# Hybrid decoder step with 32 experts: eight neighbouring weight rows per partition, low parts off GpSimd, gathers ahead of the second split

## Chip, cores and metric

The kernel runs on one core of a Trainium2 chip. The metric is the device time of one execution in microseconds (us); the median of several runs is compared. The engines are PE (TensorE matmul; PEld is its weight load), DVE (VectorE), ACT (ScalarE), POOL (GpSimd) and SP (SyncE, which here only issues transfers). Every engine works through its own queue in order.

## What is computed

One step of a one-layer decoder on 1024 prompt tokens and 64 sample tokens (1088 rows of 1024). A combined projection feeds a recurrent head group and a dilated window attention, their outputs go through `w_out`, then comes the mixture of experts that this change is about, then a gated per-layer embedding and a last norm. The reference computes the experts densely:

```python
def expert_step(acc, ws):
    wg, wu, wd, c = ws
    out = (jax.nn.silu(hf @ wg) * (hf @ wu)) @ wd
    return acc + c[:, None] * out.astype(jnp.float32), None
# hf: the 1088 normalized rows; wg, wu [1024, 256], wd [256, 1024], 32 experts
# c: non-zero for 2 experts a token (best of 4 groups, then the best 2 of its 8)
acc, _ = lax.scan(expert_step, jnp.zeros((n, D), jnp.float32), (wg, wu, wd, comb.T))
```

## The kernel before

All products are made exact enough by splitting every operand into a high and a low part (`split`: the high part is a copy on ACT, the low part `src - hi` a subtraction on another engine), and by three matmul passes high*high, high*low and low*high (`mm3`, L1283).

Stages, in order: projection and recurrent heads, attention, and then
- **phase 4** (about 960 to 1075 us of the span): nine token tiles. Each goes through `w_out`, is normalized (`norm`, L1345: `hn` is written to the table HN in DRAM, one row of 1024 per token), and routed (`route`, a chain of small DVE instructions). The last `route` ends with `idx`, the token numbers of each expert's 96 slots (L1476).
- **phase 5** (about 1088 to 1465 us): a loop over the 32 experts, software-pipelined. For expert e: `gather` (L1524, an indirect transfer issued by POOL) fetches 96 rows of HN; `xt` transposes them on PE, 128 columns at a time, and splits the result (`xh`, `xl`); `gu` multiplies by the gate and up weights (8 blocks of 128 rows, 24 matmuls into p4g); `act` (L1547 to L1549) makes silu(gate)*up; `ht` transposes and splits that (`hh`, `hl`); `down` multiplies by the down weights (12 matmuls into p4y), copies the two halves of the result out (L1568 on ACT, L1570 on DVE) and stores them to YE.
- **phase 6** (about 1460 us to the end): the rows of YE are fetched back per token, mixed, gated and written.

Weights of an expert arrive by `load_w` (gate and up, two transfers each for two halves, L1243 and L1244, into `wraw`) and `load_d` (down, one transfer, L1265, into `draw`), all issued by SP. Two experts' gate/up fit into `wraw`, four experts' down into `draw`; a load is issued when the split of the expert that held the buffer has read it. `split_w` (four quarters, `wh` on ACT, `wl` on DVE) and `split_d` (two halves, `dh` on ACT, `dl` on POOL) make the parts; both record their instructions on L47 (high) and L49 (low). `split_w` of expert 1 has an extra wait on `after_idx`, the instruction that writes `idx`. Which instruction stands where in an engine's queue is decided by a scheduler from the program order and its own estimate of durations.

In memory a gate or up matrix is 1024 rows of 1 KB. Block k of 128 rows (rows 128k to 128k+127) has its row 128k+p on partition p, so a partition receives four separate rows of 1 KB from one transfer. A down matrix has rows of 4 KB.

Of the kernel before, what the change touches and what calls it, by code (L numbers as in the profile page):

```python
# [29 lines left out]
XB = 4      # tiles of x in flight  # L30
# [3 lines left out]
class K:  # L34
# [9 lines left out]
    def split(self, hi, lo, src, lo_eng=None, hi_eng=None):  # L44
        """hi + lo == src exactly; hi and lo carry float32r values."""
        nc = self.nc
        (hi_eng or nc.scalar).activation(hi, src, AF.Copy) if (hi_eng or nc.scalar) is nc.scalar else hi_eng.tensor_copy(hi, src)  # L47
        e = lo_eng or nc.vector
        return e.tensor_tensor(lo, src, hi.bitcast(F32), op=ALU.subtract)  # L49

    def bcast_row(self, vec, n):
        """DRAM vector of n values as [128, n], the same on each partition."""
        return bass.AP(tensor=vec.tensor, offset=vec.offset, ap=[[0, 128], [1, n]])

    def rstd(self, pool, ss, n, width, eps, scale, tag):
        """(ss*scale + eps)^-0.5 for a [n, width] tile."""
# [16 lines left out]
    def dram(self):  # L73
# [3 lines left out]
        self.XV = t("XV", [4, 128, T])           # value, per pair of heads, channel-major  # L77
        self.ARd = t("ARd", [4, 128, 17, 128])   # per chunk: removal key | receptance, times the decay so far; last chunk: samples
        self.KB = t("KB", [4, 128, T])           # key over the decay so far
        self.BB = t("BB", [4, 128, T])           # removal key times a over the decay so far  # L80
        self.PC = t("PC", [4, 128, 24])          # decay over a chunk; 16 prompt chunks, 8 sequences
        self.BV = t("BV", [4, 128, T])           # bonus
# [3 lines left out]
        self.QP = t("QP", [2, 512, NP])          # prompt queries, channel-major, as an exact sum of two float32r parts  # L86
# [7 lines left out]
    def phase1(self):  # L94
        nc, tc, I, O = self.nc, self.tc, self.I, self.O
        with ExitStack() as es:
# [13 lines left out]
            # projection, 25 tiles of 128 columns, the lora tile first; the first two go along with the norm  # L110
# [33 lines left out]
            # last projected rows  # L144
# [7 lines left out]
    def vectors(self, c1):  # L152
        nc, I = self.nc, self.I
        nc.sync.dma_start(self.cst, I['cst'])
        # per-channel vectors, channel-major
# [23 lines left out]
        # mu * state_shift, [128, b, ct]  # L179
# [68 lines left out]
    def project(self, ct, out, chunks=range(3)):  # L248
        """columns 128 ct.. of the projection, channel-major; those of RWKV shifted by a token"""
# [28 lines left out]
    def copy(self, c, after):  # L278
        """Half of a sample's cache moves on, not before another instruction; the last rows come with the projection."""
# [33 lines left out]
    def lora(self, lora, lp):  # L313
        nc, I, vec, pm = self.nc, self.I, self.vec, self.pm1
        # contractions over 32 or 64 rows: the data's high and low parts stacked, the weights' parts in two passes
# [47 lines left out]
    def rwkv_ops(self, p, xr, xk, xv, ep):  # L363
        """per-token operands of a pair of heads: decay products within chunks, keys, bonus"""
# [7 lines left out]
        # decay so far within the chunk: before and after the token  # L372
# [17 lines left out]
        # removal key, normalized per head, negated  # L390
# [12 lines left out]
        # key  # L403
# [3 lines left out]
        # bonus  # L407
# [11 lines left out]
        # products with the decay  # L419
# [23 lines left out]
def host_consts():  # L443
    """Tables that depend on shapes alone."""
# [10 lines left out]
    # identity rows for a quarter of the columns: column 4c + d on partitions with (p // 8) % 4 == d  # L455
# [5 lines left out]
class K2(K):  # L461
# [17 lines left out]
    def pools2c(self, es):  # L479
        """tiles that stay over the RWKV stage and the samples' part of it"""  # L480
        nc = self.nc
        self.c2 = c2 = es.enter_context(self.pool("c2", side="right"))
        # zero-padded block-diagonal operands; the padding is written once
# [27 lines left out]
    def pools2a(self, es):  # L511
        """the first of pools2, opened while the projection still runs"""
# [28 lines left out]
    def phase2a(self):  # L541
        """the first chunks' systems, which the projection hides"""
# [48 lines left out]
    def pair_load(self, dst, src, t0, nck):  # L591
        """[pair, channel, token] into the block-diagonal [channel, chunk, pair, (head, token)]"""
# [5 lines left out]
    def prepA(self, u):  # L598
        """what the chunk systems and the states' first products need; two chunks, or the samples"""
# [71 lines left out]
    def solve(self, u, G):  # L671
        """(I - A)^-1 of each 64 x 64 chunk system: 32-row halves by forward substitution, joined by products.
        Partition (head of the pair, half, column mod 4, chunk and pair)."""
# [19 lines left out]
    def join(self, u, G):  # L693
        nc, sv, X = self.nc, self.sv, G['X']
        TT = G['TT'] = self.TT[u % 2]
        R1 = sv.tile([128, 8, 32], F32, tag="R1", name="R1")     # rows: [t, column / 4, (column mod 4, system)]
        RT = sv.tile([128, 8, 32], F32, tag="RT", name="RT")     # transposed: [column, system, t]
# [3 lines left out]
        # diagonal halves; systems of pairs 0, 1 on rows 0..63, of pairs 2, 3 on rows 64..127  # L701
# [26 lines left out]
    def solve_s(self, G):  # L728
        """inverse of the 8 x 8 systems, one per partition (pair, head, sequence)"""
# [62 lines left out]
    def sample2(self, G, y):  # L792
# [4 lines left out]
        for p in range(4):  # L797
            # states, rows (sequence parity, v), then turned to [(head, k), (sequence, v)]
# [28 lines left out]
            for j, (src, lhs) in enumerate(((G['Vt'][:, 0, p, :], G['Kt']), (u, G['Bt']))):  # L827
                # rows spread over their sequence
# [69 lines left out]
class K3(K2):  # L898
# [3 lines left out]
    def attn_out(self, pool, X, at, n, i0, gat, tags=("asq", "an", "ao"), bufs=1, w=512):  # L902
        """rmsnorm of [n, 512] mixed heads, then channel-major into MX[4:8]."""
# [59 lines left out]
    def head(self, h, ia, ib):  # L963
        """a head's operands for query tiles ia..ib"""
# [4 lines left out]
        # keys: high over low part; queries: either part twice  # L969
# [9 lines left out]
    def samples_out(self, pool, X, n, w):  # L979
        """the samples' heads, from rows per head to rows per token"""  # L980
# [13 lines left out]
    def phase3(self, pairs, depth, banks, hooks={}):  # L994
        nc, tc, I, O = self.nc, self.tc, self.I, self.O
        gat, at = self.gat, self.at
        with ExitStack() as es:
# [5 lines left out]
            else:       # stays for the following phases  # L1003
# [864 lines left out]
```

## Time and profile before

| | |
|---|---|
| time, median of 3 runs | 1621.02 us |
| the runs | 1618.59, 1621.02, 1627.01 us |
| span of the profiled execution | 1623.8 us |
| PE, DVE, ACT, POOL busy | 86%, 59%, 44%, 34% of the span |
| mean granted clock of TensorE | 0.932 of full speed |

No separate time was recorded for the profiled execution; its span, from its first to its last instruction, lies inside the range of the timed runs and 2.8 us above their median. Busy shares are averages over stages that differ; matmul ends are modelled, so a PE that is busy throughout is not at its peak.

### The profile page before, as it was taken

How to read it: one execution, taken by the hardware profiler on the slowest of the kernel's cores; microseconds unless marked ns; L12 is line 12 of the kernel's file. 1: busy time of each engine (PE TensorE's matmuls, PEld its weight loads, DVE VectorE, ACT ScalarE, POOL GpSimd, SP SyncE). 2: the span in 40 equal slices, each digit the busy share in tenths (PEclk: the TensorE clock that was granted, in tenths of full speed). 3: DMA queues.
4: the chain of work that ended last, by engine and by line, in shares of the span. 5: the costliest groups of instructions: out<-in, count | busy, mean ns of one | idle time of the engine just before them, and what ended most of it. 6: DMA issues, size and time to landing. Idle time of an engine off the chain costs nothing. (4 is left out here: it accounts for less than half of the span.)

```text
span 1623.8 us, 24626 instructions
## 1 busy us (share of the span) xinstructions
PE 1398.6 (86%) x9017; PEld 1159.6 (71%) x9018; DVE 960.8 (59%) x2121; ACT 722.2 (44%) x1304; POOL 549.1 (34%) x427
## 2 busy tenths in 40 slices
PE   4999999999889889973988999948988788797996
PEld 4888999999667767762867787836765455565884
DVE  7524663551476857343656534459876678686664
ACT  5535453231334435341444633327765566674332
POOL 8004651001122222431223513126675454454230
PEclk9999999999979898986999998979999899899998
DMA  6156558895774753366676566579999799996551
GB/s 200 53 177 188 153 164 284 301 348 179 200 219 138 190 162 115 90 138 156 202 209 187 157 212 213 188 246 319 340 364 336 241 309 319 319 348 220 189 183 65
DMA packets 306158, 350.02 MB, mean 216 GB/s; under 512 B 105757, under 2 KB 249951, under 8 KB 305504
## 3 DMA queue, kind: packets, MB, share of 16 engines
q1 hardware_dynamic: 261424, 287.46, 56.4%
q0 software_dynamic: 39712, 43.76, 9.7%
q10 hardware_dynamic: 4896, 17.17, 2.8%
q8 instruction: 73, 1.20, 0.3%
q14 instruction: 53, 0.43, 0.1%
HBM read 277.45 MB, written 104.33 MB: 235 GB/s over the span
## 5 line engine op out<-in xcount | busy, mean ns | idle before, releaser
L49 POOL TENSOR_TENSOR dl<-draw,dh 128x1024 fp32r<-128x1024 f32 x66 | 175.3, 2678 | 98.8 <-ACT dh L47 98.7
L264 PE MATMUL pj<-hT_hi,wh 128*128 128x384 f32 (+1 forms) x600 | 198.9, 333 | 4.7 <-DVE lora L272 2.7
L264 PE MATMUL pj<-hT_hi,wl 128*128 128x384 f32 (+1 forms) x600 | 198.6, 331 | 0.0
L264 PE MATMUL pj<-hT_lo,wh 128*128 128x384 f32 (+1 forms) x600 | 198.0, 330 | 0.0
L264 PEld LDWEIGHTS pj<-hT_hi,wh 128*128 128x128 f32 x600 | 113.4, 190 | 6.6 <-DVE lora L272 3.0
L264 PEld LDWEIGHTS pj<-hT_hi,wl 128*128 128x128 f32 x600 | 113.6, 189 | 2.4 <-issue 2.2
L264 PEld LDWEIGHTS pj<-hT_lo,wh 128*128 128x128 f32 x600 | 113.9, 190 | 0.6 <-issue 0.2
L47 ACT ACTIVATE dh<-draw 128x1024 fp32r<-128x1024 f32 x66 | 66.3, 1052 | 70.2 <-PE p4y L1283 41.2
L688 DVE TENSOR_TENSOR ftmp<-At,X 128x60 f32<-128x60 f32 (+24 forms) x248 | 59.3, 251 | 44.7 <-DMA At<-ABd 26.9
L1040 PE MATMUL pS<-k,q 128*128 128x512 f32 (+2 forms) x192 | 56.3, 401 | 33.6 <-DMA q<-QP 32.2
L1524 POOL DMA_INDIRECT x<-HN,idx x32 | 51.3, 1604 | 94.0 <-PE p4t L1534 37.8
L1069 PEld LDWEIGHTS po<-v,pt 128*128 128x128 f32 x576 | 74.2, 197 | 10.7 <-issue 2.4
L1069 PE MATMUL po<-v,pt 128*128 128x128 f32 x576 | 79.8, 284 | 1.4 <-ACT pt L1067 1.1
L1052 ACT ACTIVATE s<-s,nm 128x128 f32<-128x128 f32 (+7 forms) x64 | 49.4, 772 | 61.8 <-DVE X L744 21.3
L767 POOL TENSOR_TENSOR s<-S,pc 128x512 f32<-128x512 f32 x16 | 16.9, 1053 | 162.6 <-PE pj L264 69.9
L690 DVE TENSOR_TENSOR X<-X,ftmp 128x60 f32<-128x60 f32 (+24 forms) x248 | 59.0, 250 | 4.5
L49 DVE TENSOR_TENSOR wl<-w,wh 128x1024 fp32r<-128x1024 f32 x25 | 35.0, 1400 | 44.7 <-ACT wh L47 43.9
L1043 DVE CUSTOM_DVE_ANT_0 s<-pS,bias 128x512 f32<-128x512 f32 (+2 forms) x96 | 50.9, 552 | 17.7 <-PE pxt L1063 13.2
L1040 PEld LDWEIGHTS pS<-k,q 128*128 128x128 f32 x192 | 32.7, 208 | 39.9 <-issue 21.8
L1283 PE MATMUL p4y<-dh,hl 128*96 128x512 f32 x128 | 52.4, 409 | 5.5 <-DVE hl L49 5.5
L1067 ACT ACTIVATE pt<-pxt 128x512 f32<-128x512 f32 (+3 forms) x64 | 32.6, 512 | 54.7 <-PE pxt L1063 41.8
L1283 PE MATMUL p4y<-dh,hh 128*96 128x512 f32 x128 | 48.1, 416 | 5.5 <-ACT hh L47 5.3
(653 smaller groups left out, 3874.9 us busy)
## 6 DMA issues: line engine op xcount, KB each, us to landing
wraw<-in_w_gate_dram SPq DMA_DIRECT2D x64, 512.0 KB
wraw<-in_w_up_dram SPq DMA_DIRECT2D x64, 512.0 KB
draw<-in_w_down_dram SPq DMA_DIRECT2D x32, 1024.0 KB
out_dram<-in_cache_k_win_dram SPq DMA_DIRECT2D x16, 1016.0 KB
out_dram<-in_cache_v_win_dram SPq DMA_DIRECT2D x16, 1016.0 KB
w<-in_w_in_dram SPq DMA_DIRECT2D x25, 512.0 KB
kc<-in_cache_k_win_dram SPq DMA_DIRECT2D x48, 256.0 KB
vc<-in_cache_v_win_dram SPq DMA_DIRECT2D x48, 256.0 KB
```

The lines of the kernel that those rows point to most:

```text
L47: (hi_eng or nc.scalar).activation(hi, src, AF.Copy) if (hi_eng or nc.scalar) is nc.scalar else hi_eng.tensor_copy(hi, src)
L49: return e.tensor_tensor(lo, src, hi.bitcast(F32), op=ALU.subtract)
L264: nc.tensor.matmul(p[:, :nn], a[:, k, :], b[:, k, n0:n0 + nn], start=(m == 0), stop=(m == 23))
L688: nc.vector.tensor_tensor(o, At[:, t, t + 1:32][:, :, None].to_broadcast([128, m, c]), X[:, t, None, 0:c].to_broadcast([128, m, c]), op=AL ...
L690: nc.vector.tensor_tensor(X[:, t + 1:32, 0:c], X[:, t + 1:32, 0:c], o, op=ALU.add)
L1040: nc.tensor.matmul(ps[:, :n], q[:, a, i * 128:(i + 1) * 128], k[:, c0:c0 + n], start=(a == 0), stop=(a == 1))
L1043: nc.vector.tensor_tensor_reduce(s[:, c0:c0 + n], ps[:, :n], bias[:, bo:bo + n], 1.0, -3e38, ALU.add, ALU.max, m)
L1052: ex = nc.scalar.activation(s[:, :nb * 128], s[:, :nb * 128], AF.Exp, bias=nm, accum_out=den)
L1067: nc.scalar.activation(pt[:, b0:b0 + m, :], px[:, :m, :], AF.Copy)
L1069: nc.tensor.matmul(po, pt[:, b, :], v[:, b, :], start=(b == 0), stop=(b == nb - 1))
L1283: self.nc.tensor.matmul(p, a[x][:, k, :], w, start=(k == 0 and q == 0), stop=(k == kn - 1 and q == 2))
L1524: nc.gpsimd.indirect_dma_start(out=X[e][:n], out_offset=None, in_=self.HN, in_offset=bass.IndirectOffsetOnAxis(ap=self.idx[:, e:e + 1], ax ...
```

## The change

- `load_w` puts rows 8p to 8p+7 of a gate or up matrix on partition p: a transfer takes rows 8p+4g to 8p+4g+3, which are 4 KB in one piece in memory, to 4 KB in one piece on the partition. Block k of the product then holds rows 8p+k. `split_w` only views the buffer in that order.
- So that the data agree, `norm` writes `hn` with its columns permuted: column 128k+p holds channel 8p+k. The instruction reads `x2` and the gain with a step of 8 elements (32 bytes).
- `split_d` makes the low parts `dl` on DVE and not on POOL. In `down` both halves of the result are copied out by ACT; the DVE copy goes.
- `moe_start` issues the gathers of experts 0, 1 and 2 before expert 0's split in program order, and behind them a one-element memset on POOL; `split_w` of expert 1 waits for that memset and not for `idx`.
- The overflow path (`overflow_expert`, for an expert with over 96 tokens) reads its weights in the new order. Comments and docstrings that the new file leaves out are not shown.

```diff
 def load_w(self, j, after=(None, None), part=(0, 1)):
...
             if 0 <= j < NE:
-                self.hold(nc.sync.dma_start(t[:, :, 0:256], v(I['w_gate'][0, j])), after[g])
-                self.hold(nc.sync.dma_start(t[:, :, 256:512], v(I['w_up'][0, j])), after[g])
+                v = lambda a: a.rearrange("(p k) f -> p k f", k=KC)[:, 4 * g:4 * g + 4, :]
+                t = t.rearrange("p a b -> p (a b)").rearrange("p (s k f) -> p s k f", s=2, k=4)
+                self.hold(nc.sync.dma_start(t[:, 0], v(I['w_gate'][0, j])), after[g])
+                self.hold(nc.sync.dma_start(t[:, 1], v(I['w_up'][0, j])), after[g])
+                t = t.rearrange("p s k f -> p k s f")
...
 def split_w(self, j, q, eng=None, after=None):
...
-        self.hold(self.split(t[0], t[1], self.W[j][2][q // 2][:, o], lo_eng=eng), after)
+        src = self.W[j][2][q // 2][:, o]
+        h, l = (x.rearrange("p k (s f) -> p k s f", s=2) if 0 <= j < NE else x for x in t)
+        self.hold(self.split(h, l, src, lo_eng=eng), after)
...
 def split_d(self, j, k):
...
-        return self.split(h[:, k], l[:, k], r[:, k], lo_eng=self.nc.gpsimd)
+        return self.split(h[:, k], l[:, k], r[:, k])
...
 def norm(i):
...
-            nc.vector.scalar_tensor_tensor(hn[:n], x2[:n], r[:n], gf[:n], op0=ALU.mult, op1=ALU.mult)
+            v = lambda a: a[:n].rearrange("t (p k) -> t k p", k=KC)
+            nc.vector.scalar_tensor_tensor(hn[:n].rearrange("t (k p) -> t k p", k=KC), v(x2), r[:n], v(gf), op0=ALU.mult, op1=ALU.mult)
             nc.gpsimd.dma_start(self.HN[t0:t0 + n, :], hn[:n])
...
 def down(e):
...
-                if j:
-                    nc.scalar.activation(y[:n, c], p[:n], AF.Copy)
-                else:
-                    nc.vector.tensor_copy(y[:n, c], p[:n])
+                nc.scalar.activation(y[:n, c], p[:n], AF.Copy)
...
 def moe_start(self):
-        gather(0)
-        gather(1)
+        for e in range(3):
+            gather(e)
+        m = self.tc.keep_in_program_order(self.nc.gpsimd.memset(self.c4.tile([1, 1], F32, name="issued"), 0.0))
+        self.after_idx = m
         for q in range(4):
             self.split_w(0, q)
...
 def phase5(self):
...
         for e in range(NE + 1):
-            if e == 0:
-                gather(2)
```

POOL's queue at the start of phase 5: the gathers of experts 0 to 6 and the first low parts of down weights (`dl`), before:

```order
L1353 DMA HN<-hn 128x1024
L1524 DMA x_11024<-HN,idx 96x1024
L1524 DMA x_11026<-HN,idx 96x1024
L1524 DMA x_11070<-HN,idx 96x1024
L1524 DMA x_11121<-HN,idx 96x1024
L1524 DMA x_11197<-HN,idx 96x1024
L1524 DMA x_11299<-HN,idx 96x1024
L1524 DMA x_11401<-HN,idx 96x1024
L49 TENSOR_TENSOR dl<-draw,dh 128x1024 x2
```

and in the changed kernel (its L1532 is L1524 of before, L1361 is L1353):

```order
L1361 DMA HN<-hn 128x1024
L1532 DMA x_11024<-HN,idx 96x1024
L1532 DMA x_11026<-HN,idx 96x1024
L1532 DMA x_11028<-HN,idx 96x1024
L1585 MEMSET issued 1x1
L1532 DMA x_11123<-HN,idx 96x1024
L1532 DMA x_11199<-HN,idx 96x1024
L1532 DMA x_11301<-HN,idx 96x1024
L1532 DMA x_11403<-HN,idx 96x1024
```

The order of the gathers is the same; the memset stands behind the third, and from there to the end of phase 5 POOL has gathers alone. On DVE the four low parts of expert 1 (`wlb`) stand at the same place in both, behind the last `route` and ahead of expert 0's `xl`; only what they wait for has moved.

DVE's queue over one expert in the first third of phase 5, before (`wli` and `wlj`: low parts of gate/up, `y`: the copy of the first half of `down`'s result, `h`: the two products of `act`):

```order
L49 TENSOR_TENSOR xl<-p4t,xh 128x4x96
L1570 COPY y_11615<-p4y 96x512
L49 TENSOR_TENSOR wli<-wraw,whi 128x1024
L49 TENSOR_TENSOR hl<-p4h,hh 128x192
L1548 TENSOR_TENSOR h_11709<-p4g,h_11709 96x256
L49 TENSOR_TENSOR wli<-wraw,whi 128x1024
L49 TENSOR_TENSOR xl<-p4t,xh 128x4x96
L1549 TENSOR_TENSOR h_11709<-p4g,h_11709 96x256
L49 TENSOR_TENSOR wlj<-wraw,whj 128x1024 x2
```

and in the changed kernel (its L1556 and L1557 are L1548 and L1549 of before):

```order
L49 TENSOR_TENSOR xl<-p4t,xh 128x4x96
L49 TENSOR_TENSOR dl<-draw,dh 128x1024 x2
L49 TENSOR_TENSOR hl<-p4h,hh 128x192
L1556 TENSOR_TENSOR h_11711<-p4g,h_11711 96x256
L49 TENSOR_TENSOR wlj<-wraw,whj 128x1024
L1557 TENSOR_TENSOR h_11711<-p4g,h_11711 96x256
L49 TENSOR_TENSOR wlj<-wraw,whj 128x1024
L49 TENSOR_TENSOR xl<-p4t,xh 128x4x96
L49 TENSOR_TENSOR wlj<-wraw,whj 128x1024 x2
```

The copy is gone, and the two `dl` of the next expert stand ahead of `hl`, both products of `act` and the next expert's `wl`.

ACT's queue over the same expert in the changed kernel:

```order
L1575 ACTIVATE y_11617<-p4y 96x512
L47 ACTIVATE dh<-draw 128x1024 x2
L1575 ACTIVATE y_11617<-p4y 96x512
L47 ACTIVATE hh<-p4h 128x192
L1555 ACTIVATE h_11711<-p4g 96x256
L47 ACTIVATE whj<-wraw 128x1024
```

Before, only the second copy `y` stood there, behind `dh`; the rest has the same order. SP issues the same 64 + 64 + 32 weight transfers.

## Rows read from the trace of the kernel before

**Rows 1.** The page: the span, and busy us (share) and instructions of each engine.

```profile
span 1623.8 us, 24626 instructions
PE 1398.6 (86%) x9017; PEld 1159.6 (71%) x9018; DVE 960.8 (59%) x2121; ACT 722.2 (44%) x1304; POOL 549.1 (34%) x427
```

**Rows 2.** Busy time in stretches: start and end, length, busy us (instructions) of PE, PEld, DVE, ACT, POOL, granted clock, DMA share (over 1 where transfers overlap in an engine), GB/s. All of phase 5, its middle, and the 20 us that moved most.

```profile
1088.00:1465.00 377.00, 319.89 (x1482) 220.66 (x1482) 285.05 (x316) 243.31 (x349) 209.07 (x91) 0.93 0.95 315
1100.00:1440.00 340.00, 284.94 (x1320) 196.31 (x1320) 255.68 (x282) 216.72 (x314) 190.66 (x83) 0.93 0.97 320
1180.00:1200.00 20.00, 19.10 (x94) 13.38 (x93) 16.22 (x20) 12.31 (x19) 15.40 (x7) 1.00 1.07 362
```

**Rows 3.** Two lines of the instructions by line: the sigmoid of `act`, once an expert, with the start of its first and last; and the time that PE stood before the first matmul after the branch of `overflow` (PE's timeline: start, duration, instruction, idle time before it and what ended it).

```profile
L1547 ACT ACTIVATE h<-p4g x32: 363/380/383, 1098.4 to 1455.4; 96x256 f32<-96x256 f32 x32
...
1396.71 0.71 PE L1283 MATMUL p4g<-wha,xh 128*96 128x512 f32 x1 [7.63 <-DVEq L1641]
```

**Rows 4.** The DMA view of two short stretches, 1147 to 1150 us (only pieces of 1 KB) and 1310 to 1311.5 us (only pieces of 4 KB but for four): packets, MB, GB/s, and how many packets were how small.

```profile
DMA packets 1052, 1.04 MB, mean 348 GB/s; under 512 B 32, under 2 KB 1052, under 8 KB 1052
...
DMA packets 151, 0.60 MB, mean 403 GB/s; under 512 B 2, under 2 KB 4, under 8 KB 151
```

**Rows 5.** Issues of 1100 to 1460 us: transfer, queue, count, KB each. Those of `w_up` read like those of `w_gate`.

```profile
wraw<-in_w_gate_dram SPq DMA_DIRECT2D x54, 512.0 KB
draw<-in_w_down_dram SPq DMA_DIRECT2D x26, 1024.0 KB
YE<-y ACTq DMA_DIRECT2D x30, 384.0 KB
```

**Rows 6.** Groups of instructions of 1100 to 1440 us by line and shape: count, busy us and mean ns of one, idle time before.

```profile
L49 POOL TENSOR_TENSOR dl<-draw,dh 128x1024 fp32r<-128x1024 f32 x56 | 147.7, 2660 | 78.2 <-ACT dh L47 78.1
...
L49 DVE TENSOR_TENSOR wls<-wraw,whs 128x1024 fp32r<-128x1024 f32 x4 | 4.7, 1216 | 0.6 <-ACT whs L47 0.6
L49 DVE TENSOR_TENSOR xl<-p4t,xh 128x384 fp32r<-128x384 f32 x57 | 30.3, 544 | 3.2 <-ACT xh L47 3.2
L49 DVE TENSOR_TENSOR hl<-p4h,hh 128x192 fp32r<-128x192 f32 x29 | 10.1, 349 | 16.4 <-ACT hh L47 16.4
L1548 DVE TENSOR_TENSOR h<-p4g,h 96x256 f32<-96x256 f32 x29 | 11.9, 411 | 17.4 <-ACT h L1547 17.4
L1570 DVE COPY y<-p4y 96x512 f32<-96x512 f32 x28 | 19.0, 677 | 7.6 <-PE p4y L1283 7.4
...
L47 ACT ACTIVATE dh<-draw 128x1024 fp32r<-128x1024 f32 x56 | 56.2, 1052 | 53.4 <-PE p4y L1283 35.5 <-issue 17.8
L47 ACT ACTIVATE xh<-p4t 128x384 fp32r<-128x384 f32 x59 | 26.8, 483 | 3.9 <-PE p4t L1534 3.9
L1568 ACT ACTIVATE y<-p4y 96x512 f32<-96x512 f32 x28 | 16.1, 575 | 0.0
L1547 ACT ACTIVATE h<-p4g 96x256 f32<-96x256 f32 x29 | 10.9, 377 | 26.9 <-PE p4g L1283 26.8
L47 ACT ACTIVATE hh<-p4h 128x192 fp32r<-128x192 f32 x29 | 9.4, 323 | 30.8 <-PE p4h L1557 24.6 <-issue 4.6 <-PE p4t L1534 1.6
```

**Rows 7.** Timeline of phase 5 around 1124 us (start, duration, engine, instruction, idle time before it): four `dl` in a row on POOL, one `wl` on DVE, and PE's next matmul.

```profile
1123.88 9.44 POOL L49 TENSOR_TENSOR dl<-draw,dh 128x1024 fp32r<-128x1024 f32 x4
1125.59 8.81 DVE L49 TENSOR_TENSOR wlg<-wraw,whg 128x1024 fp32r<-128x1024 f32 x1
1136.66 0.74 PE L1283 MATMUL p4g<-whf,xl 128*96 128x512 f32 x1 [5.65 <-DVE xl L49]
```

**Rows 8.** What SP's queue waited for in phase 5 (total us, times, longest), and from ACT's timeline one `dh` that stood ready with nothing in the profile to wait for.

```profile
SPq L1265 <- POOL dl L49: 94.3, 20, 8.7
...
1212.03 2.01 ACT L47 ACTIVATE dh<-draw 128x1024 fp32r<-128x1024 f32 x2 [4.76 <-issue]
```

**Rows 9.** PE's work for one expert: ten matmuls of 512 columns in a row (the chain that ended last) and the eight transposes of `xt` (timeline).

```profile
1453.05 2.31 PE p4g L1283 x10
...
1202.44 0.82 PE L1534 MATMUL p4t<-ident,x 96*128 96x96 f32 x8
```

**Rows 10.** Timeline from the last tile of phase 4 to the first matmul of phase 5.

```profile
1065.30 1.28 DVE L1352 SCALAR_TENSOR_TENSOR hn<-x,r4r,gain 128x1024 f32<-128x1024 f32 x1 [0.74 <-POOL r4r L61]
1066.50 0.25 DVE L1373 SCALAR_TENSOR_TENSOR lgs<-p4h,r4r,rb 128x36 f32<-128x36 f32 x1
1074.74 4.61 DVE L49 TENSOR_TENSOR wlb<-wraw,whb 128x1024 fp32r<-128x1024 f32 x4
1075.47 4.75 POOL L1524 DMA_INDIRECT x<-HN,idx  x1 [8.03 <-DVE ci L1637]
1079.37 0.37 SPq L1243 DMA_DIRECT2D wraw<-in_w_gate_dram  x1
1080.53 0.92 POOL L1524 DMA_INDIRECT x<-HN,idx  x1 [0.31 <-issue]
1086.93 1.54 PE L1534 MATMUL p4t<-ident,x 96*128 96x96 f32 x8 [12.73 <-DMA x<-HN,idx]
1088.39 1.20 DVE L49 TENSOR_TENSOR xl<-p4t,xh 128x384 fp32r<-128x384 f32 x2 [9.04 <-ACT xh L47]
```

**Rows 11.** Two reductions on DVE in `route`: 96 elements read with a step of 8 elements, and 192 neighbouring ones (min/median/max ns).

```profile
L1397 DVE TENSOR_REDUCE rse<-rt x3: 316/323/340, 988.5 to 1068.1; 128x24 f32<-128x96 f32 x3
...
L1417 DVE TENSOR_REDUCE rrk<-rsl x3: 344/348/353, 1006.6 to 1072.3; 128x6 f32<-128x192 f32 x3
```

More of the change, by code (lines that the diff above doesn't have):

```diff
@@ L1650, in overflow_expert @@
         V = lambda t, w: r4.tile([128, w], F32, name="v" + t, tag=t, bufs=1)
-        wt = lambda n, k, m: I[n][0][ds(e, 1)].rearrange("o p f -> p (o f)")[128 * k:128 * k + 128 * m]
+        wt = lambda n: I[n][0][ds(e, 1)].rearrange("o p f -> p (o f)")
         for k in range(4):
             for q, n in ((0, 'w_gate'), (256, 'w_up')):
-                nc.sync.dma_start(g[k][:, :, q:q + 256], wt(n, 2 * k, 2).rearrange("(k p) f -> p k f", p=128))
+                nc.sync.dma_start(g[k][:, :, q:q + 256], wt(n).rearrange("(p k) f -> p k f", k=KC)[:, 2 * k:2 * k + 2])
         for k in range(2):
-            nc.sync.dma_start(d[k], wt('w_down', k, 1))
+            nc.sync.dma_start(d[k], wt('w_down')[128 * k:128 * k + 128])
         for i, (t0, n) in enumerate(TT):
```

## Prediction

> **What bounds the kernel now.** I first look for the stage. PE is busy 86% of the span [rows 1], but the edits touch phase 5, its start, and `norm` in phase 4, so I read phase 5 by itself: 377 us in which no engine is full, PE at 85%, DVE 76%, ACT 65%, POOL 55%, while the DMA engines show 0.95, and in the slice that moved most 1.07 at 362 GB/s [rows 2]. So transfers come nearest to a limit.
>
> What does an expert take? The first and last sigmoid lie 357.0 us apart, 31 experts, 11.52 us each. Once, PE stood 7.63 us for the branch of `overflow`, which the change leaves alone [rows 3]; without it 11.27 us.
>
> What must the DMA engines move for an expert? Gate and up 4 x 512 KB = 2.10 MB, down 1.05 MB, the store 0.39 MB [rows 5], and the gather as much as the store: 3.93 MB. Pieces of 1 KB went at 348 GB/s, pieces of 4 KB at 403 [rows 4]. Gate and up, in 1 KB pieces, take 2.10 / 348 = 6.03 us, the other 1.84 MB 4.55 us: 10.58 us. The measured 11.27 is 0.69 us or 6.5% more.
>
> That rest has a visible cause. POOL's `dl` and DVE's subtractions slow each other: a `wl` that takes 1.216 us where POOL is quiet [rows 6] took 8.81 us beside four `dl`, and PE then stood 5.65 us [rows 7]. DVE's work for an expert, unhindered, is 4 x 1.216 + 2 x 0.544 + 0.349 + 2 x 0.411 + 0.677 = 7.80 us [rows 6]; it was busy 255.7 us in 340 [rows 2], which at 11.52 us are 29.5 experts, 8.66 us each. So 0.86 us per expert is mutual slowing. And SP stood 94.3 us because the buffer of the next down matrix was still being read by `dl` [rows 8]; what stands behind that load in SP's queue waits too.
>
> **The change, part by part.**
>
> *Rows of 4 KB.* The bytes stay, the pieces of gate and up go from 1 KB to 4 KB. Both speeds are in [rows 4], so per expert 2.10 / 348 - 2.10 / 403 = 6.03 - 5.20 = 0.83 us less, and the DMA floor is 3.93 / 403 = 9.75 us. The bounds: nothing, if 403, seen over 1.5 us, is a burst that a whole phase doesn't sustain; 0.83 if it is sustained. I take the whole, since these were plain weight loads too. The Trainium skill, in "DMA: Bandwidth & Descriptors", section "Specifications", speaks against that twice: it puts full rate at pieces of 512 B or more, by which 1 KB pieces have nothing to gain, and a core's share of HBM at about 358 GB/s, by which the 403 would not last. On the first the trace disagrees (348 against 403); on the second the fastest 20 us, 362 GB/s, lie close to the page's figure, though they were moved largely in 1 KB pieces. By the page's figure an expert would take 10.98 us and the sum below would be about 1609 us.
>
> *Low parts from POOL to DVE, a copy from DVE to ACT.* DVE loses 0.677 and gains 2 x 1.216 us: 9.55 us an expert, now unhindered but for the gathers. ACT becomes 6 x 1.052 (`wh`, `dh`) + 2 x 0.483 + 0.377 + 0.323 + 2 x 0.575 = 9.13 us [rows 6], from 8.55. PE needs 36 matmuls of 0.231 us and eight transposes in 0.82: 9.14 us [rows 9], and two short transposes more. So the DMA floor of 9.75 is still the highest, but three engines stand within 0.7 us of it, where before the next engine stood 1.4 below 10.58. What the lock cost (0.86 us of DVE) goes; what comes is that `dl` stands in DVE's queue ahead of `hl` and `act`. Bounds for the net of the two: a gain of the whole 0.69 us above the floor, or a loss, worked out under rival C. I take it as zero: the excess over the floor stays 0.69 us, with another cause. An expert then takes 9.75 + 0.69 = 10.44 us, 0.83 less, and 31 of them 25.7 us.
>
> SP's wait for `dl` should shrink, since DVE makes it 1.2 us after `dh` and not up to 2.7 [rows 6]; that is part of the same net. The transfers that SP issues keep their number.
>
> *The start.* The first gather held POOL 4.75 us, from 1075.47 to 1080.22, during which DVE made the four `wlb`, 4.61 us; the next took 0.92 [rows 10]. In the change the gathers go first: three of 0.92 with 0.31 between them end 3.4 us after the first begins, at 1078.9, then DVE makes `wlb` until 1083.5. Behind `wlb` in DVE's queue are expert 0's `xl` and expert 2's `wl`; PE waits for `xl`. The load of expert 3, which waits for `wlb` to free its buffer, goes out some 4 us later (before: up to 1079.37) and so behind the gathers instead of beside them. Expert 0's rows were read 6.7 us after the first gather's end [rows 10]; the same from 1076.4 is 1083.1, transposes and `xh` 1.5 us more, `xl` at 1084.6 and not 1088.39. That is 3.8 us. Bounds: zero, if the 4.75 us belong to a first gather as such; 6 us if the gathers also land faster without the load beside them, less what `wlb` then costs.
>
> *The strided `hn`.* A reduction of 192 neighbouring elements took 348 ns, one of 96 with a step of 32 bytes 323 [rows 11]. With the fixed part of a short one unknown between 0 and 348 ns, the strided element costs from no more than the other up to (323 - 174) / 96 = 1.55 ns more. For 1024 elements that is 0 to 1.6 us on top of 1.28; I take 0.8, the middle. Nine times, of which eight lie under phase 4's matmuls. The last stands ahead of the last routing chain (`hn` 1065.30, `lgs` behind it at 1066.50 [rows 10]) and delays `idx` and all behind it: +0.8 us. If the other eight aren't covered, 6.4 us come on top.
>
> *At no cost.* Two pairs of `dl` in phase 4 (4 x 1.216 = 4.9 us of DVE) and the last ones beside phase 6's splits lie where PE has other matmuls and POOL's slowing of DVE goes; uncovered they cost 4.9 us. The memset, the views of `split_w` and the overflow path (not taken, or equal) cost nothing that a row could show.
>
> Sum: -25.7 - 3.8 + 0.8 = -28.7 us. From the profiled span of 1623.8 that is 1595; the span lies 2.8 us over the runs' median, so against the median of 1621.0 it is **1592 us**, -1.8%.
>
> **Rivals.**
>
> *A. PE or DVE becomes the bound and little is lost.* Without the lock the engines drop to the floor: 9.75 us an expert, 31 x 1.52 = 47 us, with the start 1571 us. For it: the whole visible cause of the excess goes [rows 7, 8]. Against: four resources at 9.1 to 9.75 us, in order, seldom all keep pace.
>
> *B. The transfers don't go faster over a whole phase.* At 362 GB/s, the best 20 us [rows 2], an expert takes 10.86 us at the least; if only the lock's excess goes, 31 x 0.41 = 13 us, with the start 1605 us. This is the mechanism of the page's figure for HBM. If neither packets nor lock give anything, only the start is left: 1618 us, no difference that a measurement tells.
>
> *C. DVE's queue stalls behind `dl`.* ACT's `dh` waited 53.4 us in 340 for matmuls or for weights that hadn't landed [rows 6, 8], 1.81 us per expert. `dl` now makes DVE wait along with it, and `hl`, `act` and the next `wl` stand behind. With the 17.4 us that DVE already waits for the sigmoid (0.59 each) an expert takes 9.55 + 1.81 + 0.59 = 11.95 us: 31 x 0.68 = 21 us more, 1639 us. It decides from 11.27 - 9.55 = 1.72 us of DVE waits per expert. Against: ACT stood at the same place before, with `hh` and the sigmoid behind it, and most of DVE's work hung on ACT anyway; and faster loads shorten the wait.
>
> **Chances and range.** The forecast (1577 to 1604) 0.46; A 0.20; B at about 1605 0.14, with nothing gained 0.09; C 0.11. The range 1567 to 1617 leaves out C and the ends of A and of the forecast, about 2 in 10. A difference of 0.5%, 8 us, is about what a measurement of this kernel can tell. Faster than 1613 are the forecast, A and most of B: 0.81. Within 8 us: 0.10. Slower: 0.09.
>
> **What would show it.** Right: SP's gate/up loads at about 400 GB/s in packets of 4 KB; first to last sigmoid near 331 us, 7.6 of them the branch; every `wl` and `dl` on DVE at about 1.2 us; the first gather near 0.9 us and the first `xl` near 1085; `hn` at about 2 us. Wrong: DVE idle behind `dh` with PE waiting for `hl` or `wl` (C); DMA share over 1 at 360 GB/s with pieces of 4 KB (B); PE without idle time (A).

## The result, and the profile after

The changed kernel took 1574.77 us (median of 4 runs, 1571.74 to 1575.35) against 1624.01 for the kernel before on the same chip: a ratio of 0.9696, 95% interval 0.9662 to 0.9731. The forecast was 1592 us and a range of 1567 to 1617. So the time lies inside the range, 17 us below the forecast; how much of the reasoning held is another matter, and most of this part is about that. In one run below (half of the pieces on POOL) one execution of four was a slow one of 3345.7 us, and the median given there is that of the other three.

The page of the changed kernel (span; busy us, share and instructions of each engine; compare [rows 1]), and behind it its phase 5 in the three stretches that matter below (columns as in [rows 2]):

```profile
span 1570.0 us, 24571 instructions
PE 1382.5 (88%) x9017; PEld 1152.6 (73%) x9018; DVE 960.4 (61%) x2155; ACT 738.1 (47%) x1336; POOL 369.8 (24%) x362
```

```profile
1100.00:1207.00 107.00, 107.00 (x540) 76.94 (x539) 96.32 (x124) 89.56 (x135) 24.83 (x12) 1.00 1.03 385
1207.00:1310.00 103.00, 87.77 (x393) 59.46 (x392) 76.58 (x93) 70.74 (x104) 9.89 (x9) 0.92 0.97 342
1310.00:1406.00 96.00, 88.61 (x432) 62.40 (x430) 81.73 (x104) 74.82 (x112) 7.36 (x5) 0.96 0.98 375
```

The sigmoid of `act` by line with its first and last start, and on PE's timeline the first matmul behind the branch of `overflow` (compare [rows 3]; L1555 is L1547 of before):

```profile
L1555 ACT ACTIVATE h<-p4g x32: 361/378/395, 1091.2 to 1405.4; 96x256 f32<-96x256 f32 x32
...
1351.43 0.71 PE L1289 MATMUL p4g<-wha,xh 128*96 128x512 f32 x1 [6.06 <-DVEq L1647]
```

First to last sigmoid is 314.2 us, not 357.0. The span fell by 53.8 us, and 42.8 of them lie here. The rest: 3.7 us up to the last `hn`, 3.5 from there to the first sigmoid, 3.8 behind the last sigmoid. Without the branch an expert takes (314.2 - 6.06) / 31 = 9.94 us; 11.27 before, 10.44 forecast.

Read by single sigmoids, that mean hides two paces. Sigmoids 1 to 14, 14 to 22 and 22 to 32 came every 10.0, 15.1 and 10.7 us before (the branch is in the last ten), and every 8.9, 12.8 and 9.6 after. In the first stretch of the changed kernel PE has no idle time at all (107.00 of 107); in the middle it stands 15 us of 103, and its granted clock there is 0.92 on average.

The groups by line that answer to [rows 6], of 1080 to 1440 us:

```profile
L49 DVE TENSOR_TENSOR dl<-draw,dh 128x1024 fp32r<-128x1024 f32 x62 | 73.2, 1221 | 32.9 <-ACT dh L47 32.7
L49 DVE TENSOR_TENSOR wlg<-wraw,whg 128x1024 fp32r<-128x1024 f32 x8 | 9.5, 1217 | 0.0
L47 ACT ACTIVATE dh<-draw 128x1024 fp32r<-128x1024 f32 x62 | 62.2, 1052 | 9.5 <-PE p4y L1289 9.4
```

No low part is stretched any more: the same `wlg` of which one took 8.81 us [rows 7] takes 1.217 in the mean. ACT's `dh`, which waited 53.4 us [rows 6], waits 9.5. The start, from the timeline (compare [rows 10]):

```profile
1072.63 1.00 POOL L1532 DMA_INDIRECT x<-HN,idx  x1 [7.86 <-DVE ci L1643]
1073.94 0.93 POOL L1532 DMA_INDIRECT x<-HN,idx  x1 [0.30 <-issue]
1075.17 0.91 POOL L1532 DMA_INDIRECT x<-HN,idx  x1 [0.30 <-issue]
1076.08 0.09 POOL L1585 MEMSET issued<- 1x1 f32 x1
1076.20 4.63 DVE L49 TENSOR_TENSOR wlb<-wraw,whb 128x1024 fp32r<-128x1024 f32 x4 [4.29 <-POOL issued L1585]
1079.11 1.54 PE L1542 MATMUL p4t<-ident,x 96*128 96x96 f32 x8 [7.82 <-DMA x<-HN,idx]
1080.75 1.02 DVE L49 TENSOR_TENSOR xl<-p4t,xh 128x384 fp32r<-128x384 f32 x2
```

What SP's queue waited for in phase 5 (compare [rows 8]; the down loads now wait for `dl` 25.6 us and not 94.3):

```profile
SPq L1271 <- DVE hl L49: 32.7, 14, 10.1
SPq L1271 <- DMA wraw<-in_w_up_dram: 27.1, 12, 3.8
SPq L1271 <- DVE dl L49: 25.6, 6, 6.6
```

### The profile page after: what moved, and what is told of

Its sections match the earlier page's. It is cut to its first block, busy times and chain, and to the rows that moved or that the text cites. A ratio compares the mean times of both kernels' runs of the same rounds, so it can differ in the third digit from the quotient of the medians.

```text
span 1570.0 us, 24571 instructions
## 1 busy us (share of the span) xinstructions
PE 1382.5 (88%) x9017; PEld 1152.6 (73%) x9018; DVE 960.4 (61%) x2155; ACT 738.1 (47%) x1336; POOL 369.8 (24%) x362
## 5 line engine op out<-in xcount | busy, mean ns | idle before, releaser
L1532 POOL DMA_INDIRECT x<-HN,idx x32 | 49.9, 1560 | 255.2 <-PE p4t L1542 154.1
L49 DVE TENSOR_TENSOR dl<-draw,dh 128x1024 fp32r<-128x1024 f32 x66 | 78.0, 1221 | 43.8 <-ACT dh L47 43.6
```

The costliest lines, as they stand in the source:

```text
L1532: nc.gpsimd.indirect_dma_start(out=X[e][:n], out_offset=None, in_=self.HN, in_offset=bass.IndirectOffsetOnAxis(ap=self.idx[:, e:e + 1], ax ...
```

## The experiments

Times are medians; the ratio is to the kernel before, run on the same chip beside each group (1620.9, 1619.1 and 1620.0 us for the three groups). "Version without rows" is the changed kernel with the layout of gate and up, the strided `hn` and the overflow path of before.

### One part at a time

**Rows alone.** The kernel before with the diff's hunks of `load_w`, `split_w`, `norm` and `overflow_expert`.

> The kernel before with one edit: gate and up in rows of 4 KB (with the strided hn and the overflow path that belong to it); low parts, copy and gathers stay as before. Theory T, the transfers bind an expert and the engines' mutual slowing adds a rest: 31 experts lose 0.83 us each (25.7 us), the strided hn costs about 1, so about 1600 us against 1624. Rival L, the slowing of POOL and DVE binds and transfers only seem full: the four dl beside the subtractions stay, so the time falls by less than 8 us. Rival S, neither binds by itself, and the parts are worth more together than apart: between 8 and 20 us.

Measured: 1628.5 us, ratio 1.0070 (1.0037 to 1.0103): slower by less than 1%. Its sigmoids:

```profile
L1553 ACT ACTIVATE h<-p4g x32: 361/380/382, 1108.9 to 1466.5; 96x256 f32<-96x256 f32 x32
```

357.6 us, as before. The largest term of the forecast, 25.7 us, is not there. So theory T is refuted for the kernel before.

**Low parts alone.** The hunks of `split_d` and `down`.

> The kernel before with one edit: low parts of the down matrices on DVE and both copies of y on ACT; gate and up in pieces of 1 KB, gathers as before. Theory T: the floor of 10.58 us an expert from 1 KB pieces stays, so at most the 0.69 us above it go, 31 x 0.69 = 21 us, and some 4 us in phase 4; by the excess of 0.19 us seen after the change 31 x 0.50 = 15.5 us and 4, about 1604 us, with first to last sigmoid near 341 us. Rival L: 35 us or more, about 1589 or below, and first to last sigmoid at 331 us or less.

Measured: 1588.9 us, ratio 0.9815 (0.9758 to 0.9872): 32 us faster. Sigmoids 328.8 us apart, 28.2 less, more than T allowed and less than L's 331 asked for. The group of `wlg` on DVE, which is back at its unhindered time, and PE's waits for low parts (total us, times, longest):

```profile
L49 DVE TENSOR_TENSOR wlg<-wraw,whg 128x1024 fp32r<-128x1024 f32 x8 | 9.5, 1217 | 0.0
```

```profile
PE p4g L1283 <- DVE xl L49: 2.4, 3, 0.9
PE p4y L1283 <- DVE hl L49: 1.3, 2, 0.7
```

In the kernel before the same waits of PE were longer, and low parts of gate and up (here `wlv`) stood among the longest:

```profile
PE p4g L1283 <- DVE xl L49: 8.0, 3, 5.7
...
PE p4g L1283 <- DVE wlv L49: 6.9, 2, 6.6
PE p4y L1283 <- DVE hl L49: 5.5, 3, 2.6
```

One thing rides along that the diff doesn't show: with `dl` on DVE the scheduler puts the matmuls of `down` one half of `gu` later in PE's queue, so the two-line edit is also a new order on PE, DVE and ACT.

**Gathers alone.** The hunks of `moe_start` and `phase5`.

> The kernel before with one edit: the first three gathers ahead of expert 1's split, with the memset that the split waits for. By the prediction's step the first sigmoid comes 3.8 us earlier and nothing else changes, so 1620 us against 1624, and the first gather takes about 1 us, not 4.75. Rival: phase 5 is bound by transfers already under way, and what is won at the first expert is waited for again by the next ones, so no difference.

Measured: 1620.8 us, ratio 1.0006 (0.9972 to 1.0039). The first gather took 1.00 us. From the last `hn` to the first sigmoid it was 4 us shorter (29.1, before 33.1), as the step had it; from first to last sigmoid 357.9 us, 0.9 more. No net gain, as the rival said. But the rival's reason, that transfers bind the phase, isn't borne out: read one by one, the 31 intervals between sigmoids of this run and those of rows alone lie within 0.4 us of those of the kernel before, although pieces of 1 KB went faster here (379 GB/s, shown further down) and rows alone kept the DMA engines less busy (share 0.90 from 1100 to 1400 us, before 0.96). So the rate of the transfers did not set the pace of the kernel before.

**All but the rows.**

> The changed kernel with the row layout taken back (1 KB pieces, hn in its natural order), everything else kept. Theory T: the floor of 10.58 us an expert returns; with an excess of 0.19 us that is 31 x 0.83 = 25.7 us more than 1575, less about 1 for hn: about 1600 us. Rival L: within 8 us of 1575. Rival S: 30 us or more above 1575, since each part alone gives little.

Measured: 1563.8 us, ratio 0.9686 (0.9631 to 0.9741), against 0.9696 of the whole change. T is refuted here too: with pieces of 1 KB the phase took 316.5 us from first to last sigmoid (314.2 in the second run below), with pieces of 4 KB 314.2. So the low parts and the gathers make the gain: -32 alone, 0 alone, and -57 together.

### Does the row layout cost anything?

> The changed kernel once more, to stand beside the next three on one chip. Theory H, the row layout's price is the strided hn, which runs longer in phase 4 and ahead of the last routing: 8 to 12 us slower than the version without rows. Rival N, the 11 us between the two so far come from the two chips and from stretches of a lower clock in phase 4: within 4 us of it.

> The changed kernel without the row layout, once more: by theory H 8 to 12 us faster than the changed kernel, by rival N within 4 us of it. The 31 experts between first and last sigmoid took 316.5 us in it and 314.2 in the changed kernel, so a difference above 2 us has to lie ahead of phase 5.

The third is the changed kernel with the old line in `norm`:

```diff
-            nc.vector.scalar_tensor_tensor(hn[:n].rearrange("t (k p) -> t k p", k=KC), v(x2), r[:n], v(gf), ...)
+            nc.vector.scalar_tensor_tensor(hn[:n], x2[:n], r[:n], gf[:n], ...)
```

> The changed kernel with hn written in its natural order; the columns of hn then don't stand in the order that the rows of gate and up need, so the experts' results are not the reference's, while every size, order and byte stays. By theory H it drops to about 2 us below the version without rows, some 10 us below the changed kernel; each hn takes 1.28 us again and not 2.18. By the prediction's step only the last hn counts, 0.9 us. By rival N no difference either.

Measured: 1574.3 (ratio 0.9723, 0.9688 to 0.9758), 1568.6 (0.9671, 0.9633 to 0.9708) and 1568.5 us (0.9681, 0.9645 to 0.9718). The medians stand as theory H has them, with 6 us and not 10; the intervals overlap, so this group alone doesn't show it. The strided `hn` of the changed kernel, by line:

```profile
L1360 DVE SCALAR_TENSOR_TENSOR hn<-x,r4r,gain x7: 2055/2185/2304, 982.5 to 1061.6; 128x1024 f32<-128x1024 f32 x7
```

and in the version with the old line:

```profile
L1359 DVE SCALAR_TENSOR_TENSOR hn<-x,r4r,gain x7: 1280/1285/1285, 983.3 to 1061.0; 128x1024 f32<-128x1024 f32 x7
```

0.9 us each, nine times. That the layout costs some 6 to 8 us is shown where it was added to the kernel before (1.0070, interval above 1); that the strided `hn` is the whole of it fits and isn't shown.

### What the low parts cost on POOL

The version without rows, with work on POOL that nobody waits for (`wr` is a dead tile):

```diff
                     self.split_d(e + 1, k)
+                    if e + 1 < NE:
+                        wr = self.router[0].rearrange("p k c -> p (k c)")[:, 0:256]
+                        for _ in range(4):
+                            nc.gpsimd.tensor_tensor(wr, wr, wr, op=ALU.subtract)
```

> The changed kernel without the row layout, in which POOL, for experts 2 to 31, subtracts 8 pieces of 256 columns of a dead tile, as many elements as the low parts had, and nobody waits for it; the order of the other engines' work is nearly that of the version without it. If the mutual slowing of POOL and DVE was the loss (theory L), DVE's subtractions stretch again, 0.86 us an expert, and the time rises by 15 to 27 us. If the loss was the waits behind the low parts (the down buffers that SP waited for) and the order in which the engines take the work, it rises by less than 8 us.

Measured: 1634.2 us, ratio 1.0090 (1.0062 to 1.0117), 65.6 us above the version without it, more than any theory said. The groups by line:

```profile
L1618 POOL TENSOR_TENSOR wrt<-wrt 128x256 f32<-128x256 f32 x224 | 244.1, 1090 | 16.2
L49 DVE TENSOR_TENSOR dl<-draw,dh 128x1024 fp32r<-128x1024 f32 x52 | 71.1, 1407 | 36.5 <-ACT dh L47 36.5
```

And from PE's waits (total us, times, longest):

```profile
PE p4t L1534 <- DMA x<-HN,idx: 47.6, 9, 11.1
```

The dose was too high: a piece took 1.09 us, so POOL was busy 244 us where the low parts of before took 147.7 [rows 6], and the gathers stood behind the pieces in POOL's queue. DVE's `dl` is stretched (1.407 against 1.221), but 47.6 us of the loss are late gathers; 18 remain. Hence the same with `range(2)`:

> Like the run in which POOL subtracts pieces that nobody waits for, with half of them: 4 pieces of 256 columns an expert, 1.09 us each as measured there, 4.4 us of POOL an expert against 5.3 of the low parts before. There PE stood 47.6 us for gathers that stood behind the pieces in POOL's queue; with half, that wait should be below 15 us. If the mutual slowing by itself costs, 10 us or more remain beyond that wait and DVE's subtractions of 1024 columns stay above 1.3 us in the mean; if it doesn't, the time is that of the version without pieces within 8 us, beyond the wait for gathers.

Measured: 1605.8 us, ratio 0.9901 (0.9872 to 0.993), 37 to 42 us above the two medians without it. The same two groups, and the same wait of PE behind them:

```profile
L1618 POOL TENSOR_TENSOR wrt<-wrt 128x256 f32<-128x256 f32 x108 | 129.1, 1195 | 7.7
L49 DVE TENSOR_TENSOR dl<-draw,dh 128x1024 fp32r<-128x1024 f32 x58 | 74.8, 1330 | 31.2 <-ACT dh L47 31.2
```

```profile
PE p4t L1534 <- DMA x<-HN,idx: 32.4, 7, 8.8
```

One of these seven waits is that of the phase's first matmul, which the version without pieces has as well. Here, and there (second run):

```profile
1083.75 1.54 PE L1534 MATMUL p4t<-ident,x 96*128 96x96 f32 x8 [7.47 <-DMA x<-HN,idx]
```

```profile
1079.89 1.54 PE L1534 MATMUL p4t<-ident,x 96*128 96x96 f32 x8 [7.67 <-DMA x<-HN,idx]
```

So late gathers cost 25 us, and not below 15: the pieces, which wait for nothing, run ahead in blocks. Taken off, 12 to 17 us remain by the medians. Between first and last sigmoid it is less: 349.2 us, against 314.2 and 316.5 without pieces, leaves 8 to 10. So two-input work on POOL, even if nobody needs it, costs some 8 to 18 us besides the gathers that it delays; the half dose by itself stands at the bound of 10 us that was set for it. That is a quarter to a half of the 32 us of the low parts; the rest (SP's wait for `dl`, 94.3 us [rows 8] and 23.2 with the low parts alone moved, and the new order on PE) was not taken apart: the run that moved `dl` changed the order too.

### What the gathers are worth

> The version without rows, with the three gathers first but without the memset that the split of expert 1 waited for; every engine takes its work in the same order. The low parts alone gave 1589 us, with the gathers and the wait 1564 to 1569, though the gathers and the wait alone gave nothing. If the wait (no DVE subtraction beside the first gather) is what counts, about 1585 and a first gather of 4.7 us; if the order of the gathers counts, about 1568.

The edit is the two lines of the memset taken out of `moe_start`. Measured: 1587.1 us, ratio 0.9783 (0.9753 to 0.9813), the time of the low parts alone. So the order of the gathers is worth nothing, and the wait, which keeps DVE's `wlb` away from the first gather, some 20 us, of which 12 to 15 lie between first and last sigmoid (328.9 us, against 316.5 and 314.2 with the wait). Its first gather on the timeline, and its busy time, clock, DMA share and GB/s from 1100 to 1220 us:

```profile
1074.15 4.76 POOL L1524 DMA_INDIRECT x<-HN,idx  x1 [8.02 <-DVE ci L1632]
```

```profile
1100.00:1220.00 120.00, 116.09 (x583) 82.31 (x582) 103.88 (x134) 96.15 (x148) 26.60 (x14) 1.00 1.06 354
```

The version without rows, with the wait (second run), over the same stretch:

```profile
1100.00:1220.00 120.00, 119.06 (x599) 85.53 (x597) 106.19 (x138) 98.04 (x148) 26.75 (x14) 1.00 1.06 378
```

Both have the DMA engines full (1.06), but one moves 354 GB/s and the other 378. It is the same in stretches that hold only pieces of 1 KB. Low parts alone, 1100 to 1103 us:

```profile
DMA packets 1009, 1.00 MB, mean 334 GB/s; under 512 B 31, under 2 KB 1009, under 8 KB 1009
```

The same view without rows, with the wait, and then of gathers alone, both from 1106 to 1109 us:

```profile
DMA packets 1135, 1.13 MB, mean 377 GB/s; under 512 B 31, under 2 KB 1135, under 8 KB 1135
```

```profile
DMA packets 1132, 1.14 MB, mean 379 GB/s; under 512 B 37, under 2 KB 1131, under 8 KB 1131
```

It lasts. Low parts alone from 1306 to 1309 us, and without rows, with the wait (first run), from 1351 to 1354 us:

```profile
DMA packets 1057, 1.05 MB, mean 350 GB/s; under 512 B 32, under 2 KB 1057, under 8 KB 1057
```

```profile
DMA packets 1169, 1.16 MB, mean 385 GB/s; under 512 B 40, under 2 KB 1169, under 8 KB 1169
```

In the three kernels with 1 KB pieces in which `wlb` and the first gather collide (before, low parts alone, without the wait) no stretch of 3 us with such pieces alone went above 362 GB/s; with the wait (gathers alone and both runs without rows) the fastest reach 386 to 391, though slower ones occur there too (351 GB/s in the second run without rows, from 1246 to 1249 us). So the 348 GB/s of [rows 4], which the forecast read as the speed of 1 KB pieces, is the speed that they have after one kind of start. Whether the collision itself makes the difference isn't shown, for the wait moves something else too: it holds back `wlb`, and with it the loads that need its buffer. Without the wait SP issued the next two loads of `w_gate` ahead of the second gather (1079.22 us), at

```profile
1075.79 0.38 SPq L1243 DMA_DIRECT2D wraw<-in_w_gate_dram  x1
1078.06 0.37 SPq L1243 DMA_DIRECT2D wraw<-in_w_gate_dram  x1
```

and with it (second run) the first of them at 1079.43 us, behind all three gathers. No run separates the two, and why either should slow transfers for the next 300 us stays open. The Trainium skill, "DMA: Bandwidth & Descriptors", section "SWDGE vs HWDGE vs iDMA", says that the descriptors of POOL's transfers are written into SBUF state which DVE locks POOL out of while DVE runs in its two-port mode; the first gather (4.76 us beside `wlb`, 1.00 without) looks like such a hold, but no run here shows in which mode `wlb`, a subtraction with two inputs, ran, nor what it does to the transfers after it.

### What binds the changed kernel

Both start from the version without rows. In the first, `gu` leaves out the pass of `xl` with `wh`:

> The version without rows, with gate and up in two matmul passes instead of three (the low part of x times the high part of the weights is left out of the experts' results): 28 matmuls of 0.231 us an expert and not 36, 1.85 us less PE work. In the changed kernel the experts outside the middle eight went by every 8.9 us, about what PE needs, the middle eight every 12.8. If PE binds the outer 23 experts and nothing stands behind it, they win up to 1.8 us each, some 40 us. If the transfers (366 GB/s over the phase) bind the phase as a whole, the middle waits longer for what the ends win, and it is less than 8 us.

Measured: 1559.3 us, ratio 0.9628 (0.959 to 0.9666), 5 to 9 us less than the version without rows, mostly inside the intervals. Its stretch, against the first of the changed kernel above:

```profile
1100.00:1207.00 107.00, 88.56 (x414) 59.16 (x413) 88.98 (x118) 81.63 (x126) 28.03 (x13) 0.94 1.06 385
```

PE has 18 us less to do, the transfers run at the same 385 GB/s, and the sigmoids come no faster (every 9.5 us over the first 13 intervals, 8.9 with three passes). The scheduler changed the order of work on PE, DVE and ACT with this edit. In the second, `load_d` of an odd expert from 5 on hands out the tile of the expert before:

```diff
+        if j < NE and j % 2 and j > 3:
+            self.Dn[j] = self.rd
+            return
```

> The version without rows, in which the odd experts from 5 on take the down matrix of the expert before them: 14 loads of 1.05 MB fewer, all other work as before (the results of those experts are wrong). That is 14.7 MB, 40 us at 366 GB/s. If transfers bind the phase, the time falls by 20 us or more, as far as PE's pace of 8.9 us an expert lets it: 31 x (10.1 - 8.9) less the 6 us of the branch is some 31 us. If the middle eight are slow because of the order in which the engines take their work, it falls by less than 8 us.

Measured: 1540.1 us, ratio 0.9517 (0.9482 to 0.9553), 24 to 29 us below the version without rows. Sigmoids 14 and 22 on ACT's timeline, and 300 us of the phase by busy time:

```profile
1198.43 0.39 ACT L1550 ACTIVATE h<-p4g 96x256 f32<-96x256 f32 x1
...
1273.13 0.39 ACT L1550 ACTIVATE h<-p4g 96x256 f32<-96x256 f32 x1
```

```profile
1100.00:1400.00 300.00, 288.13 (x1411) 206.69 (x1410) 264.33 (x332) 242.80 (x361) 63.67 (x30) 0.98 0.97 332
```

The middle eight take 9.3 us each, 12.8 in the changed kernel, and PE is busy 288 us of 300. So with fewer loads of down weights the middle keeps the pace of the rest, while less work for PE hardly helped. The likely reading is that the first experts run on weights loaded ahead, PE keeps up with them, and the middle pays when that lead is used up.

That the amount of transfers binds the middle isn't shown, for their order is a rival. In the middle of the changed kernel SP issued the down loads two in a row, where the run without the odd ones had single loads:

```profile
1223.21 5.86 SPq L1271 DMA_DIRECT2D draw<-in_w_down_dram  x2
1249.21 6.51 SPq L1271 DMA_DIRECT2D draw<-in_w_down_dram  x2
1273.11 7.40 SPq L1271 DMA_DIRECT2D draw<-in_w_down_dram  x2
```

Each pair falls into a long interval: from sigmoid 15 on they are 18.0, 7.4, 18.9, 6.8, 19.3 and 6.4 us. And the longest waits of PE between 1207 and 1310 us ended with a high part from ACT, which stands behind `dh` in ACT's queue, not with a transfer:

```profile
PE p4g L1289 <- ACT whr L47: 3.8, 1, 3.8
PE p4g L1289 <- ACT wht L47: 3.3, 1, 3.3
```

The edit took away the pairs along with the bytes, and the scheduler moved part of the order on PE, DVE and ACT with it, so amount and order are not separated.

## Why the prediction was right, and where it wasn't

**The DMA floor (10.58 to 9.75 us): wrong, and the step that failed.** It took a speed for 1 KB pieces from one stretch of 3 us and one for 4 KB from 1.5 us [rows 4] and put the difference down to the size. The runs show that the same pieces of 1 KB go at 334 GB/s or at 377, depending on how the phase starts, and that the kernel before kept its pace at either rate. Over 300 us the changed kernel moved 366 GB/s and the version without rows 365. From first to last sigmoid the layout changed nothing (314.2 and 316.2 us with it, 316.5 and 314.2 without), so the term is 0, not -25.7 us. The Trainium skill's rule in "DMA: Bandwidth & Descriptors", "Specifications", that pieces of 512 B or more have full rate, was set aside by that comparison; the experiments agree with the rule. The 358 GB/s that the Trainium skill gives there for a core, by which the forecast doubted its own 403, did not hold as a limit either: 366 GB/s were moved over 300 us here.

**The lock, net zero: wrong.** The cause was named (POOL and DVE, [rows 7, 8]), but its price was bounded by the 0.69 us above a floor that wasn't one. Moving the low parts alone gave 32 us, and 28.2 of it between the sigmoids, 0.91 us an expert. The gain sat in the term that was set to nothing, and the term that was set to 25.7 us held none; that the two errors nearly cancel, by luck, is why the time still fell into the range.

**The start, -3.8 us: right in place, wrong in worth.** The first gather took 1.00 us (0.92 forecast). The first `xl` came at 1080.75, 3.9 us before the forecast's 1084.6, of which 3.7 are phase 4's earlier end. Alone this gain is lost again by the next experts; with the low parts moved the wait is worth some 20 us, together with a higher rate of transfers, which no step foresaw.

**The strided `hn`, 2.08 us: 2.19 measured.** The layout cost more than the +0.8 us on the path: 7.6 us in rows alone, of which phase 4 accounts for 1 to 3 (below) and the rest isn't traced.

**Phase 4 at zero: mis-sized.** From the first to the last wait ahead of `hn`, the profiles of the four kernels with the low parts on POOL or DVE and `hn` plain or strided are 108.2 us (before), 111.3 (rows alone), 103.4 (low parts alone) and 104.7 (changed): `dl` on DVE gains some 5 to 7 us, the strided `hn` costs 1 to 3. Two profiles of the version without rows differ by 2.9 us there (98.3 and 101.2), so the smaller figure lies within the spread of single profiles.

**The rivals.** A's time (1571) came, but not its mechanism: less work for PE hardly helped. B's mechanism, a rate that the phase doesn't exceed, fits the changed kernel best (366 GB/s over 300 us), with the rival of the loads' order left open; its time came out too high, since B let the lock give back only 0.41 us an expert and it gave 0.91. C did not happen as a loss: DVE does wait 32.7 us for `dh` ahead of `dl`, but ACT's `dh` waits 9.5 us, not 53.4. Bare of the row layout the change is faster still by the medians (1563.8 and 1568.6 against 1574.8 and 1574.3); the intervals don't separate them.

## What to carry to other kernels

A rate read in a stretch of a few microseconds is the rate of that state of the queues; before it becomes a term, find two stretches of the same pieces that differ in what else was going on. A mutual slowing of two engines that is visible in the trace can't be priced by the distance to a floor that was itself estimated; here a run without it gave the price. And an average over a phase hides lead: look at the intervals one by one, since a phase can run at PE's pace at its start and well below it in its middle.

## What the runs showed of the hardware that was not expected

A collision of one gather with four subtractions on DVE (4.76 us instead of 1.00) goes with 1 KB transfers that stay at or below 362 GB/s over the rest of the phase, where they reach 386 without it; whether the collision or the order of the transfers at that start does it isn't shown. Pieces of 4 KB don't hold their speed either: in the changed kernel, of two stretches of 3 us at 1165 and 1261 us, both with the DMA engines full, the first moved

```profile
DMA packets 336, 1.28 MB, mean 427 GB/s; under 512 B 23, under 2 KB 23, under 8 KB 336
```

and the second

```profile
DMA packets 235, 0.86 MB, mean 288 GB/s; under 512 B 24, under 2 KB 24, under 8 KB 235
```

What slows the second is open. A multiply on DVE over 1024 columns in steps of 32 bytes took 2.19 us where neighbouring ones took 1.285.
